# State-space products of two blocks in one group, and gate logits as one fp32r pass over stacked rows

## The chip, the core and the metric

The kernel runs on one core of a Trainium2 chip. The time is device microseconds of one execution. Five engines work side by side, each through its own list of instructions in order: TensorE (PE, matmuls), VectorE (DVE), ScalarE (ACT), GpSimd (POOL) and SyncE (SP, which issues most of the transfers).

## The reference, cut to what matters

Two layers over 256 positions of width 1024. The first layer projects its input and mixes two branches: a state-space branch (16 heads of 64, decays within chunks of 128) and a gated linear attention (8 heads, chunks of 64). The second layer is causal softmax attention, since with 256 positions no earlier block exists to be chosen. A final rms norm closes it. All arithmetic is float32.

```python
# state-space branch, layer 1
seg = a_t[..., :, None] - a_t[..., None, :]
decay_ij = jnp.exp(jnp.where(causal, seg, -jnp.inf))
y_diag = jnp.einsum('bcgeij,bcjgep->bcigep', cb[:, :, :, None] * decay_ij, xdt)
y = y_diag + y_off + d_skip[:, :, None] * x_c
# gate of the linear attention, layer 1: gate_lr is 256 x 16, gate_w2 is 16 x 512
log_decay = jax.nn.log_sigmoid(gate_lr @ gate_w2 + gate_b) / GLA_GATE_NORMALIZER
```

## The kernel before, in words

**Gemms.** Each weight piece comes by one transfer from SP into a raw tile `r_` (four buffers, `wraw`), is rounded to fp32r by ACT as `h_` (L78), and DVE takes the rest `l_ = r_ - h_` (L79). A product of float32 accuracy is then three fp32r passes, `mm3`: high by high, high by low, low by high. The tile of a gemm is named by its stage: `pa` (time-major part of layer 1, weights `wa`), `pb` (blocks of 128 features, weights `wb`), `pc` (output projection), `pv`, `pp`, `pf` (layer 2). The input `xT` is scaled and split the same way into `hhi` and `hlo`, one kb (128 of the 1024 inner rows) at a time. Since a raw tile has four buffers, the transfer of the fifth piece waits until the first piece has been read by DVE, and so on: `r_b8`, the ninth piece, waits for `l_a4`.

**Order.** PE's list is written by hand: coroutines (`co_pair`, `co_first`, `co_gla`) sleep for a number of nanoseconds of a virtual clock (`DL`, advanced by `spend`) and their small matmuls are put between two passes of the running gemm when their time has come. On ACT, DVE, POOL and SP a scheduler of the framework sets the order.

**State-space pairs.** `co_pair(blk)` handles one block of 128 features (two heads). It transposes the block (`xtp`), DVE multiplies by dt (`xdt`), `ab` spreads the cumulated decays over 128 partitions, ACT makes the decays `e` (two Relu operations per head, one Exp), POOL cuts the triangle and DVE multiplies by `cbT`. After a second delay come the products `yp`: eight passes of a 128x64 array shape, since they run in plain float32 (two passes for each of four calls) and the two heads fill 64 columns each. DVE then writes `y` from `yp`. The attention of layer 2 has products of the same shapes, `ao`, in which two pairs share one tile.

**Gate.** `co_first` transposes the 16 gate columns (`gtp`) into `glT` (DVE) and later multiplies: `lg0` and `lg1`, four passes each, from 16 rows. Around `lg0` stand `act` (two transposes from 16 rows) and `cb` (from 64 rows).

**PSUM.** The small tiles (`pm`: `xtp`, `ab`, `yp`, `lg`, `gs`, ...) share a pool of four banks. A new tile takes the bank that a reader has left, so its first matmul waits for the reads of an earlier tile.

Of the kernel before, what the change touches and what calls it, by code (L numbers as in the profile page):

```python
# [9 lines left out]
F32 = mybir.dt.float32  # L10
F32R = mybir.dt.float32r
# [14 lines left out]
AHEAD = 4  # L26

DL = {"ss": 1350, "rb": 5000, "gt": 1500, "ac": 7300, "act": 2600, "lg": 2150, "ln": 2250, "cb": 12400,
      "pair0": 11900, "pair1": 9700, "gla0": 650, "glagap": 3650, "gla1": 3350, "gla2": 8700, "r2": 10000,
      "turn": 4150, "rb1": 4000, "at0": 2600, "at2": 5000, "at1": 3700, "at3": 1800, "gqk": 250}  # L30


# [14 lines left out]
def trunk(ctx, tc, xT_d, x_d, cst_d, mat_d, gw2_d, fn_d, wa_d, wb_d, wc_d, wv_d, wp_d, wf_d, out_d):  # L47
# [132 lines left out]
    xT = big.tile([P, KB, T], F32, name="xT", tag="xT")  # L180
    cst = cpool.tile([P, C_N], F32, name="cst")
    mat = cpool.tile([P, M_N], F32, name="mat")
    gw2 = big.tile([16, 512], F32, name="gw2", tag="s4")
    nc.scalar.dma_start(cst, cst_d)
    j = 0
    for k0, n_ in CUTS_A0:
# [2 lines left out]
            raws.append(fetch(src, kbs, cols, "_".join(str(q_) for q_ in k_)))  # L189
        j += 1  # L190
    nc.sync.dma_start(mat, mat_d)
    nc.sync.dma_start(gw2, gw2_d)

    ident = mat[:, M_ID:M_ID + P]
    tri = [mat[:, M_TRI + P * i:M_TRI + P * i + P] for i in range(2)]
# [113 lines left out]
    ahl = cpool.tile([P, T], F32R, name="ahl")  # L309
    sel = cpool.tile([P, 16], F32R, name="sel")  # L310
    G.memset(ahl.bitcast(F32), 0.0)
    glT = cpool.tile([16, T], F32, name="glT")
    gab = big.tile([P, 4, T], F32, name="gab", tag="s0")
    gmn = big.tile([P, 4, T], F32, name="gmn", tag="s1")
    gcs = big.tile([P, 16, 64], F32, name="gcs", tag="s2")
# [2 lines left out]
    def co_first(ps):  # L318
# [45 lines left out]
        for b2 in range(2):  # L364
            lg = pm(f"lg{b2}")
            for j in range(2):
                b = 2 * b2 + j
                mm(lg[:, j * T:j * T + T], gw2[:, b * P:b * P + P], glT)
            for j in range(2):
                b = 2 * b2 + j  # L370
                gbc = cst[:, C_GB + b:C_GB + b + 1]
                S.activation(gab[:, b, :], lg[:, j * T:j * T + T], AF.Abs, bias=gbc)
                V.tensor_scalar(gmn[:, b, :], lg[:, j * T:j * T + T], gbc, 0.0, op0=ALU.add, op1=ALU.min)
            yield DL["lg"]
# [16 lines left out]
    def co_conv(blk, ps):  # L391
        while "rb" not in env:
            yield 100
        pd = pads[blk % 2]
        V.tensor_tensor(pd[:, 4:4 + T], ps, rb, op=ALU.mult)
        u = tmp.tile([P, T], F32, name=f"cu{blk}", tag="t1a")
        w = lambda i: cwh[:, 4 * blk + i:4 * blk + i + 1]
        S.activation(u, pd[:, 4:4 + T], AF.Identity, scale=w(3), bias=cwh[:, 40 + blk:41 + blk])
        for i in range(3):
            V.scalar_tensor_tensor(u, pd[:, 1 + i:1 + i + T], w(i), u, op0=ALU.mult, op1=ALU.add)  # L400
        th = tmp.tile([P, T], F32, name=f"cth{blk}", tag="t1b")
        S.activation(th, u, AF.Tanh)
        dst = xs[:, blk, :] if blk < 8 else bc[:, blk - 8, :]
        V.scalar_tensor_tensor(dst, th, 1.0, u, op0=ALU.add, op1=ALU.mult)
        if blk < 8:
            spawn(co_pair(blk))
        elif blk == 9:
            spawn(co_cb())

# [11 lines left out]
            S.activation(sb, ps[:, 0:3 * P], AF.Copy)  # L421
            cbT.append(sb)

    def co_pair(blk):
        yield DL["pair0"]
        tp = pm(f"xtp{blk}")
        for tt in range(2):
            tr(tp[:, tt * P:tt * P + P], xs[:, blk, tt * P:tt * P + P])
        xdt = tmp.tile([P, 2, 2, 64], F32, name=f"xdt{blk}", tag="t1c")
        V.tensor_tensor(xdt, tp[:, 0:T].rearrange("p (a b c) -> p a b c", a=2, b=2),  # L430
                        dt[:, :, 2 * blk:2 * blk + 2][:, :, :, None].to_broadcast([P, 2, 2, 64]), op=ALU.mult)
        e = tmp.tile([P, 2, 3, P], F32, name=f"e{blk}", tag="t3")
        for j in range(2):
            h = 2 * blk + j
            ab = pm(f"ab{h}")
            mm(ab[:, 0:T], sel[:, h:h + 1].to_broadcast([P, P]), ahl)
            S.activation(e[:, j, 0:2, :].rearrange("p a b -> p (a b)"), ab[:, 0:T], AF.Relu, scale=-1.0,
                         bias=acs[:, 0, h:h + 1])
            S.activation(e[:, j, 2, :], ab[:, P:T], AF.Relu, scale=-1.0, bias=acs[:, 1, h:h + 1])
        ef = e.rearrange("p a b c -> p (a b c)")  # L440
        S.activation(ef, ef, AF.Exp, scale=-1.0)
        for j in range(2):
            G.affine_select(out=e[:, j, 0:3:2, :], in_=e[:, j, 0:3:2, :], pattern=[[0, 2], [1, P]],
                            compare_op=ALU.is_ge, fill=0.0, base=0, channel_multiplier=-1)
        V.tensor_tensor(e, e, cbT[blk // 4].rearrange("p (a b) -> p a b", a=3)[:, None, :, :].to_broadcast([P, 2, 3, P]),
                        op=ALU.mult)
# [3 lines left out]
        for j, r in enumerate(rows):  # L450
            mm(yp[r, 0:T], xdt[:, 0, j, :], e[:, j, 0:2, :].rearrange("p a b -> p (a b)"), True, False)
        for j, r in enumerate(rows):
            mm(yp[r, P:T], xdt[:, 1, j, :], e[:, j, 2, :], False, True)
        V.scalar_tensor_tensor(y[:, blk, :], xs[:, blk, :], cst[:, C_DS + blk:C_DS + blk + 1], yp[:, 0:T],
                               op0=ALU.mult, op1=ALU.add)
# [451 lines left out]
```

## Time and profile before

| | |
|---|---|
| median of 3 runs | 346.22 us (346.11 to 346.32) |
| profiled execution, its own time | 345.89 us |
| span, first to last instruction | 344.2 us |
| PE busy | 334.2 us (97%) |
| DVE busy | 262.4 us (76%) |
| ACT busy | 217.4 us (63%) |
| POOL busy | 51.3 us (15%) |

Busy is the time in which an engine had at least one instruction under way. The span leaves out what lies ahead of the first and behind the last instruction, 1.7 us of the execution's own time. Matmuls are pipelined: what one costs is the step from its start to the start of the next, not its length.

### The profile page before, as it was taken

The page shows a single profiled execution, that of the slowest core. Times are in us where ns is not written, and L with a number is a line of the kernel's source. Part 1 is how long each engine was busy: PE and PEld are TensorE (multiplying, and loading weights), DVE is VectorE, ACT ScalarE, POOL GpSimd, SP SyncE. Part 2 cuts the span into 40 slices and gives each one's busy share as a digit, 9 for nine tenths or more (in the row PEclk, how much of TensorE's full clock was granted, in tenths as well). Part 3 has the DMA queues.
Part 4 walks back from the last instruction along what each step waited for, and adds up shares of the span by engine and source line. Part 5 has one row for each costly group of instructions (what it writes and reads, how often), then busy time and mean ns, then how long its engine had stood idle before and what let it go on. Part 6 is the DMA issues. An engine that isn't in the chain of part 4 may idle for free.

```text
span 344.2 us, 6316 instructions
## 1 busy us (share of the span) xinstructions
PE 334.2 (97%) x2352; PEld 306.3 (89%) x2352; DVE 262.4 (76%) x548; ACT 217.4 (63%) x445; POOL 51.3 (15%) x62
## 2 busy tenths in 40 slices
PE   7989999999999999999999999999999999999992
PEld 6989899998999899999888888899998999998792
DVE  4979999999989667789965765556867968778352
ACT  5547789898765757677542766464674856746331
POOL 2540001112405442534210000000000000000000
PEclk9999999999999999999999999999999999999998
DMA  6978673366572744631686435747544364430003
GB/s 187 268 245 299 229 231 100 89 181 174 161 238 97 263 129 168 204 92 39 202 285 239 164 134 193 237 154 235 171 150 155 120 186 127 138 109 0 2 8 115
DMA packets 17631, 56.09 MB, mean 163 GB/s; under 512 B 2096, under 2 KB 4144, under 8 KB 17472
## 3 DMA queue, kind: packets, MB, share of 16 engines
q1 hardware_dynamic: 16880, 53.53, 48.8%
q10 hardware_dynamic: 720, 2.16, 1.9%
q8 instruction: 18, 0.29, 0.3%
q14 instruction: 13, 0.11, 0.1%
HBM read 54.63 MB, written 1.05 MB: 162 GB/s over the span
## 4 chain that ended last, share of the span: by engine, by line
PE 85%; DVE 4%; issue 4%; DMA 3%; POOL 2%; ACT 1%; SPq 1%; POOLq 0%; DVEq 0%
PE pp L159 20%; PE pb L159 18%; PE pc L159 13%; PE pa L159 11%; PE pv L159 6%; PE pf L159 4%; DMA r_a<-in_wa 3%; PE yp L159 2%; PE ao L159 2%; PE as L159 2%; PE ptp L163 2%; PE gs L159 1%; PE go L159 1%; POOL rr L538 1%; POOL sT L518 1%
## 5 line engine op out<-in xcount | busy, mean ns | idle before, releaser
L159 PE MATMUL pb<-hhi,h_b 128*128 128x256 f32 x208 | 60.0, 288 | 0.0
L159 PE MATMUL pb<-hhi,l_b 128*128 128x256 f32 x208 | 58.9, 283 | 0.8 <-DVE l_b L79 0.8
L159 PE MATMUL pb<-hlo,h_b 128*128 128x256 f32 x208 | 58.8, 282 | 0.0
L159 PE MATMUL pp<-h1hi,h_p 128*128 128x256 f32 x192 | 55.5, 289 | 0.0
L159 PE MATMUL pp<-h1lo,h_p 128*128 128x256 f32 x192 | 54.3, 283 | 0.0
L159 PE MATMUL pp<-h1hi,l_p 128*128 128x256 f32 x192 | 54.3, 283 | 0.0
L79 DVE TENSOR_TENSOR l_p<-r_p,h_p 128x1024 fp32r<-128x1024 f32 x24 | 29.4, 1223 | 18.0 <-ACT h_p L78 17.7
L159 PEld LDWEIGHTS pb<-hhi,h_b 128*128 128x128 f32 x208 | 39.7, 191 | 1.2 <-issue 1.1
L159 PEld LDWEIGHTS pb<-hhi,l_b 128*128 128x128 f32 x208 | 39.8, 191 | 1.0 <-DVE l_b L79 1.0
L159 PEld LDWEIGHTS pb<-hlo,h_b 128*128 128x128 f32 x208 | 39.8, 191 | 0.0
L159 PEld LDWEIGHTS pp<-h1hi,h_p 128*128 128x128 f32 x192 | 36.7, 191 | 1.1 <-issue 0.5
L159 PEld LDWEIGHTS pp<-h1lo,h_p 128*128 128x128 f32 x192 | 36.8, 192 | 0.0
L159 PEld LDWEIGHTS pp<-h1hi,l_p 128*128 128x128 f32 x192 | 36.7, 191 | 0.0
L79 DVE TENSOR_TENSOR l_b<-r_b,h_b 128x1024 fp32r<-128x1024 f32 x26 | 33.0, 1276 | 1.8 <-ACT h_b L78 1.8
L78 ACT ACTIVATE h_p<-r_p 128x1024 fp32r<-128x1024 f32 x24 | 25.4, 1057 | 13.8 <-PE pp L159 7.4
L78 ACT ACTIVATE h_b<-r_b 128x1024 fp32r<-128x1024 f32 x26 | 27.4, 1067 | 8.0 <-DMA r_b<-in_wb 5.6
L159 PE MATMUL pa<-l_a,hhi 128*128 128x416 f32 x80 | 28.9, 361 | 1.3 <-DVE l_a L79 1.3
L159 PE MATMUL pa<-h_a,hhi 128*128 128x416 f32 x80 | 29.6, 370 | 0.0
L159 PE MATMUL pa<-h_a,hlo 128*128 128x416 f32 x80 | 28.7, 359 | 0.0
L79 DVE TENSOR_TENSOR l_a<-r_a,h_a 128x832 fp32r<-128x832 f32 (+1 forms) x24 | 22.4, 945 | 2.4 <-ACT h_a L78 2.4
L78 ACT ACTIVATE h_a<-r_a 128x832 fp32r<-128x832 f32 (+1 forms) x24 | 18.7, 783 | 8.0 <-DMA r_a<-in_wa 6.5
L79 DVE TENSOR_TENSOR l_c<-r_c,h_c 128x1024 fp32r<-128x1024 f32 x16 | 19.9, 1252 | 5.0 <-ACT h_c L78 4.9
(241 smaller groups left out, 804.2 us busy)
## 6 DMA issues: line engine op xcount, KB each, us to landing
r_b<-in_wb SPq DMA_DIRECT2D x26, 512.0 KB, 4.3
r_p<-in_wp SPq DMA_DIRECT2D x24, 512.0 KB, 4.0
r_c<-in_wc SPq DMA_DIRECT2D x16, 512.0 KB, 4.0
r_a<-in_wa SPq DMA_DIRECT2D x16, 416.0 KB, 3.7
r_v<-in_wv SPq DMA_DIRECT2D x8, 512.0 KB, 4.4
r_f<-in_wf SPq DMA_DIRECT2D x8, 512.0 KB, 3.6
r_a<-in_wa SPq DMA_DIRECT2D x8, 208.0 KB, 4.0
xT<-in_xT SPq DMA_DIRECT2D x8, 128.0 KB, 3.8
```

The costliest lines, as they stand in the source:

```text
L78: S.activation(hi, raw, AF.Copy)
L79: V.tensor_sub(lo, raw, hi.bitcast(F32))
L159: TE.matmul(out, lhsT, rhs, start=start, stop=stop)
L163: TE.transpose(out, in_, ident)
L518: G.affine_select(out=sT[:, 0:3:2, :], in_=sT[:, 0:3:2, :], pattern=[[0, 2], [1, P]], compare_op=ALU.is_ge, fill=0.0, base=0, channel_mult ...
L538: G.tensor_tensor(rr, ss, mhalf, op=ALU.pow)
```

## The change

Blocks are now taken in pairs, (0,1), (2,3), (5,4) and (6,7), by the order in which they come. Each pair is prepared block after block (`xtp`, `ab`, `e`), and the eight calls of both (16 passes) then stand in one group on one tile `yp`; the tags of `xdt` and `e` get a third buffer. The gate logits are one fp32r pass per 128 columns: rows 0 to 15 hold the high part of the gate input, rows 32 to 47 its low part, rows 64 to 79 the high part again, against high, high and low weights; the other rows are zero. For that the weights `gw2` are loaded three times from ACT's queue, behind a memset by POOL, and no longer once from SP's. `rb1` uses the tile of `rb`.

```diff
-      "pair0": 11900, "pair1": 9700, ...
+      "pair0": 6100, "pair1": 5200, "pair2": 9700, ...
...
-    gw2 = big.tile([16, 512], F32, name="gw2", tag="s4")
+    gw2 = big.tile([P, 512], F32, name="gw2", tag="s4")
...
-    nc.sync.dma_start(gw2, gw2_d)
+    G.memset(gw2, 0.0)
+    for r0 in (0, 32, 64):
+        nc.scalar.dma_start(gw2[r0:r0 + 16, :], gw2_d)
...
-    glT = cpool.tile([16, T], F32, name="glT")
+    gl3 = cpool.tile([P, T], F32R, name="gl3")
+    gw3 = big.tile([P, 512], F32R, name="gw3", tag="s2")
+    G.memset(gl3.bitcast(F32), 0.0)
...
-        V.tensor_copy(glT, gtp[0:16, 0:T])
+        S.activation(gl3[0:16, :], gtp[0:16, 0:T], AF.Copy)
+        S.activation(gl3[64:80, :], gtp[0:16, 0:T], AF.Copy)
+        V.tensor_sub(gl3[32:48, :], gtp[0:16, 0:T], gl3[0:16, :].bitcast(F32))
+        S.activation(gw3, gw2, AF.Copy)
+        V.tensor_sub(gw3[64:80, :], gw2[64:80, :], gw3[64:80, :].bitcast(F32))
...
-                mm(lg[:, j * T:j * T + T], gw2[:, b * P:b * P + P], glT)
+                mm(lg[:, j * T:j * T + T], gw3[:, b * P:b * P + P], gl3)
...
-            spawn(co_pair(blk))
+            if "xs" in env:
+                spawn(co_pair(env.pop("xs"), blk))
+            else:
+                env["xs"] = blk
...
-    def co_pair(blk):
-        yield DL["pair0"]
+    def co_pair(*blks):
...
+        for i, blk in enumerate(blks):
+            yield DL[f"pair{i}"]
...
-        yield DL["pair1"]
-        yp = pm(f"yp{blk}")
...
+        yield DL["pair2"]
+        yp = pm(f"yp{blks[0]}")
+        for n, (e, xdt) in enumerate(zip(es, xds)):
+            for j, r in enumerate(rows):
+                mm(yp[r, n * T:n * T + T], xdt[:, 0, j, :], e[:, j, 0:2, :].rearrange("p a b -> p (a b)"), True, False)
+            for j, r in enumerate(rows):
+                mm(yp[r, n * T + P:n * T + T], xdt[:, 1, j, :], e[:, j, 2, :], False, True)
```

How it moves instructions is seen at three places. On PE, the products of block 1 stood alone with the preparation of block 3 behind them (`xtp_998`, `ab_1004`, `ab_1008`; the number behind a name tells tiles apart):

```order
421 L159 MATMUL pb_976<-hlo,h_b_826 128x256
422 L159 MATMUL pb_976<-hhi,l_b_827 128x256
423 L159 MATMUL yp_992<-e_848,xdt_846 64x256 x2
424 L159 MATMUL yp_992<-e_848,xdt_846 64x128 x2
425 L163 MATMUL xtp_998<-mat,xs 128x128 x2
426 L159 MATMUL ab_1004<-ahl,sel 128x256
427 L159 MATMUL ab_1008<-ahl,sel 128x256
428 L159 MATMUL pb_976<-hhi,h_b_826 128x256
```

Now those of blocks 0 and 1 stand together, ahead of the same preparation:

```order
435 L159 MATMUL pb_1019<-hhi,l_b_886 128x256
436 L159 MATMUL yp_1026<-e_767,xdt_765 64x256 x2
437 L159 MATMUL yp_1026<-e_767,xdt_765 64x128 x2
438 L159 MATMUL yp_1026<-e_860,xdt_858 64x256 x2
439 L159 MATMUL yp_1026<-e_860,xdt_858 64x128 x2
440 L163 MATMUL xtp_1037<-mat,xs 128x128 x2
441 L159 MATMUL ab_1043<-ahl,sel 128x256
442 L159 MATMUL ab_1047<-ahl,sel 128x256
443 L159 MATMUL pb_1019<-hhi,h_b_885 128x256
```

The group of block 0, which stood alone some 60 rows earlier, is gone from there. Behind the preparation of block 3 come 24 passes of `pb` and then the preparation of block 5 (`xtp_1087`); before, 45 passes and a group of products stood between the two:

```order
465 L159 MATMUL pb_1080<-hlo,h_b_925 128x256
466 L159 MATMUL pb_1080<-hhi,l_b_926 128x256
467 L163 MATMUL xtp_1087<-mat,xs 128x128 x2
468 L159 MATMUL ab_1093<-ahl,sel 128x256
469 L159 MATMUL ab_1097<-ahl,sel 128x256
```

Four banks hold `yp_1026`, `xtp_1037`, `ab_1043` and `ab_1047`. The program has `xtp_1087` wait for ACT's reads of `ab_1043`, `ab_1093` for those of `ab_1047`, and `ab_1097` for the second `y` from `yp_1026`.

The third place is the start, on DVE, where the scheduler's order differs. Before (`hhi` and `hlo` are the split input, `l_a_4` the fifth weight piece's low part):

```order
5 L324 TENSOR_SCALAR cwh<-cst 128x50
6 L216 SCALAR_TENSOR_TENSOR hlo<-xT,cst,hhi 128x256
7 L79 TENSOR_TENSOR l_a_0_155<-r_a_0_113,h_a_0_154 128x416
8 L216 SCALAR_TENSOR_TENSOR hlo<-xT,cst,hhi 128x256
9 L79 TENSOR_TENSOR l_a_1_161<-r_a_1_116,h_a_1_160 128x416
10 L215 TENSOR_SCALAR hhi<-xT,cst 128x256
11 L79 TENSOR_TENSOR l_a_2_167<-r_a_2_119,h_a_2_166 128x416
12 L216 SCALAR_TENSOR_TENSOR hlo<-xT,cst,hhi 128x256 x2
13 L79 TENSOR_TENSOR l_a_3_173<-r_a_3_122,h_a_3_172 128x416
14 L215 TENSOR_SCALAR hhi<-xT,cst 128x256
15 L79 TENSOR_TENSOR l_a_4_179<-r_a_4_125,h_a_4_178 128x416
16 L216 SCALAR_TENSOR_TENSOR hlo<-xT,cst,hhi 128x256 x2
```

And now:

```order
6 L218 SCALAR_TENSOR_TENSOR hlo<-xT,cst,hhi 128x256
7 L217 TENSOR_SCALAR hhi<-xT,cst 128x256
8 L79 TENSOR_TENSOR l_a_0_158<-r_a_0_113,h_a_0_157 128x416
9 L218 SCALAR_TENSOR_TENSOR hlo<-xT,cst,hhi 128x256
10 L79 TENSOR_TENSOR l_a_1_164<-r_a_1_116,h_a_1_163 128x416
11 L218 SCALAR_TENSOR_TENSOR hlo<-xT,cst,hhi 128x256
12 L79 TENSOR_TENSOR l_a_2_170<-r_a_2_119,h_a_2_169 128x416
13 L218 SCALAR_TENSOR_TENSOR hlo<-xT,cst,hhi 128x256
14 L79 TENSOR_TENSOR l_a_3_176<-r_a_3_122,h_a_3_175 128x416
15 L217 TENSOR_SCALAR hhi<-xT,cst 128x256
16 L218 SCALAR_TENSOR_TENSOR hlo<-xT,cst,hhi 128x256 x2
17 L79 TENSOR_TENSOR l_a_4_182<-r_a_4_125,h_a_4_181 128x416
```

The `hhi` of the third kb (row 7, from the third `xT` transfer) now stands ahead of `l_a_0`, and the two `hlo` of row 16 stand ahead of `l_a_4`, where they stood behind it. On SP's queue the third `xT` transfer now waits for a transfer counter that `cst` used (the three `gw2` loads use three of the eight counters), where it waited for nothing, and `mat` is issued ahead of `r_b8` and `r_b9` instead of behind them.

## Rows read from the trace of the kernel before

**Rows 1.** The page: busy us of each engine, its share of the span, instructions.

```profile
PE 334.2 (97%) x2352; PEld 306.3 (89%) x2352; DVE 262.4 (76%) x548; ACT 217.4 (63%) x445; POOL 51.3 (15%) x62
```

**Rows 2.** What PE waited for: us in total, times, longest.

```profile
PE pa L159 <- DVE l_a L79: 1.3, 2, 0.7
...
PE pb L159 <- DVE l_b L79: 0.8, 1, 0.8
```

**Rows 3.** PE's timeline around one block's products (start us, us, engine, line, operation).

```profile
63.59 0.28 PE L159 MATMUL pb<-hhi,l_b 128*128 128x256 f32 x1
63.80 0.87 PE L159 MATMUL yp<-e,xdt 128*64 128x256 f32 x8
64.60 0.39 PE L159 MATMUL pb<-hhi,h_b 128*128 128x256 f32 x1
64.82 0.28 PE L159 MATMUL pb<-hlo,h_b 128*128 128x256 f32 x1
64.94 0.28 PE L159 MATMUL pb<-hhi,l_b 128*128 128x256 f32 x1
```

**Rows 4.** PE's timeline in layer 2, around products of two pairs in one group.

```profile
258.24 0.28 PE L159 MATMUL pp<-h1hi,l_p 128*128 128x256 f32 x1
258.45 1.52 PE L159 MATMUL ao<-pT,va 128*64 128x256 f32 x16
259.90 0.39 PE L159 MATMUL pp<-h1hi,h_p 128*128 128x256 f32 x1
260.13 0.28 PE L159 MATMUL pp<-h1lo,h_p 128*128 128x256 f32 x1
```

**Rows 5.** PE's timeline around the second pair of gate logits.

```profile
44.91 0.28 PE L159 MATMUL pb<-hhi,l_b 128*128 128x256 f32 x1
45.11 1.12 PE L159 MATMUL lg<-glT,gw 16*128 16x256 f32 x4
46.17 0.38 PE L159 MATMUL pb<-hhi,h_b 128*128 128x256 f32 x1
46.39 0.28 PE L159 MATMUL pb<-hlo,h_b 128*128 128x256 f32 x1
```

**Rows 6.** PE's timeline around the first pair of gate logits.

```profile
41.81 0.29 PE L361 MATMUL act<-mat,acT 16*128 16x16 f32 x2
41.96 1.10 PE L159 MATMUL lg<-glT,gw 16*128 16x256 f32 x4
42.99 0.93 PE L159 MATMUL cb<-bc 64*128 64x256 f32 x8
```

**Rows 7.** SP's queue at the start (a row's length is that of its issues).

```profile
2.65 0.43 SPq L187 DMA_DIRECT2D xT<-in_xT  x1
...
11.02 3.45 SPq L72 DMA_DIRECT2D r_b<-in_wb  x2
```

**Rows 8.** DVE's timeline at the start; in brackets the idle time before, and its releaser.

```profile
3.96 0.35 DVE L215 TENSOR_SCALAR hhi<-xT,cst 128x256 fp32r<-128x256 f32 x1 [2.75 <-DMA cst<-in_cst]
...
4.35 0.49 DVE L216 SCALAR_TENSOR_TENSOR hlo<-xT,cst,hhi 128x256 fp32r<-128x256 f32 x1
...
10.91 2.69 DVE L216 SCALAR_TENSOR_TENSOR hlo<-xT,cst,hhi 128x256 fp32r<-128x256 f32 x2
...
17.31 3.97 DVE L79 TENSOR_TENSOR l_b<-r_b,h_b 128x1024 fp32r<-128x1024 f32 x2
```

**Rows 9.** The page's groups: busy, mean ns, idle before; the low parts of all `b` pieces.

```profile
L79 DVE TENSOR_TENSOR l_b<-r_b,h_b 128x1024 fp32r<-128x1024 f32 x26 | 33.0, 1276 | 1.8 <-ACT h_b L78 1.8
```

**Rows 10.** PE's timeline, the `ab` pair of block 3.

```profile
73.42 0.48 PE L159 MATMUL ab<-ahl,sel 128*128 128x256 f32 x2
```

**Rows 11.** ACT's timeline: first and last of the four reads of that pair.

```profile
76.71 0.46 ACT L437 ACTIVATE e<-ab,acs 128x256 f32<-128x256 f32 x1
...
77.67 0.38 ACT L439 ACTIVATE e<-ab,acs 128x128 f32<-128x128 f32 x1
```

**Rows 12.** DVE's timeline: `y` of the products that stand ahead of that pair.

```profile
76.27 0.48 DVE L454 SCALAR_TENSOR_TENSOR y<-xs,cst,yp 128x256 f32<-128x256 f32 x1
```

More of the change, by code (lines that the diff above doesn't have):

```diff
@@ L28 @@
 DL = {"ss": 1350, "rb": 5000, "gt": 1500, "ac": 7300, "act": 2600, "lg": 2150, "ln": 2250, "cb": 12400,
-      "pair0": 11900, "pair1": 9700, "gla0": 650, "glagap": 3650, "gla1": 3350, "gla2": 8700, "r2": 10000,
+      "pair0": 6100, "pair1": 5200, "pair2": 9700, "gla0": 650, "glagap": 3650, "gla1": 3350, "gla2": 8700, "r2": 10000,
       "turn": 4150, "rb1": 4000, "at0": 2600, "at2": 5000, "at1": 3700, "at3": 1800, "gqk": 250}
@@ L422, in co_cb @@
             cbT.append(sb)
-    def co_pair(blk):
-        yield DL["pair0"]
[L426 to L446, printed above, removed]
-        yield DL["pair1"]
-        yp = pm(f"yp{blk}")
-        rows = [slice(64 * j, 64 * j + 64) for j in range(2)]
[L450 to L455, printed above, removed]
@@ new lines, in co_pair @@
+    def co_pair(*blks):
+        rows = [slice(64 * j, 64 * j + 64) for j in range(2)]
+        es, xds = [], []
+        for i, blk in enumerate(blks):
+            yield DL[f"pair{i}"]
+            tp = pm(f"xtp{blk}")
+            for tt in range(2):
+                tr(tp[:, tt * P:tt * P + P], xs[:, blk, tt * P:tt * P + P])
+            xdt = tmp.tile([P, 2, 2, 64], F32, name=f"xdt{blk}", tag="t1c", bufs=3)
+            V.tensor_tensor(xdt, tp[:, 0:T].rearrange("p (a b c) -> p a b c", a=2, b=2),
+                            dt[:, :, 2 * blk:2 * blk + 2][:, :, :, None].to_broadcast([P, 2, 2, 64]), op=ALU.mult)
+            e = tmp.tile([P, 2, 3, P], F32, name=f"e{blk}", tag="t3", bufs=3)
+            for j in range(2):
+                h = 2 * blk + j
+                ab = pm(f"ab{h}")
+                mm(ab[:, 0:T], sel[:, h:h + 1].to_broadcast([P, P]), ahl)
+                S.activation(e[:, j, 0:2, :].rearrange("p a b -> p (a b)"), ab[:, 0:T], AF.Relu, scale=-1.0,
+                             bias=acs[:, 0, h:h + 1])
+                S.activation(e[:, j, 2, :], ab[:, P:T], AF.Relu, scale=-1.0, bias=acs[:, 1, h:h + 1])
+            ef = e.rearrange("p a b c -> p (a b c)")
+            S.activation(ef, ef, AF.Exp, scale=-1.0)
+            for j in range(2):
+                G.affine_select(out=e[:, j, 0:3:2, :], in_=e[:, j, 0:3:2, :], pattern=[[0, 2], [1, P]],
+                                compare_op=ALU.is_ge, fill=0.0, base=0, channel_multiplier=-1)
+            V.tensor_tensor(e, e, cbT[blk // 4].rearrange("p (a b) -> p a b", a=3)[:, None, :, :]
+                            .to_broadcast([P, 2, 3, P]), op=ALU.mult)
+            es.append(e)
+            xds.append(xdt)
+        yield DL["pair2"]
[5 more added lines that the diff above has]
+                mm(yp[r, n * T + P:n * T + T], xdt[:, 1, j, :], e[:, j, 2, :], False, True)
+        for n, blk in enumerate(blks):
+            V.scalar_tensor_tensor(y[:, blk, :], xs[:, blk, :], cst[:, C_DS + blk:C_DS + blk + 1],
+                                   yp[:, n * T:n * T + T], op0=ALU.mult, op1=ALU.add)
@@ L660, in trunk @@
     rq = cpool.tile([P, 2], F32, name="rq")
-    rb1 = cpool.tile([P, T], F32, name="rb1")
+    rb1 = rb
     def co_norm():
@@ L756, in trunk @@
                 ps = gemm_fm(("p", 3 * pr + i), h1hi, h1lo, f"pp{pr}_{i}")
-                t_ = tmp.tile([P, T], F32, name=f"qk{pr}_{i}", tag=("t1a", "t1c")[i])
+                t_ = tmp.tile([P, T], F32, name=f"qk{pr}_{i}", tag=("t1a", "t1c")[i], bufs=2 + i)
                 n_ = (P, T)[i]
```

## The prediction

> **What bounds the kernel now.** I read the page's busy times first: PE has an instruction under way for 334.2 us of the 344.2 us span, 97%, the next engine is DVE with 76% [rows 1]. Then the waits of PE, since a busy engine can still be a late one: in all it waits 1.3 us for `l_a` (twice) and 0.8 us for `l_b` (once) [rows 2], and these lie in the first 20 us, where weights arrive one by one. From there on the kernel is as long as PE's list. So whatever the change takes out of PE's list is a gain, whatever it adds to DVE, ACT and POOL costs nothing as long as PE does not come to wait for it, and the two places where it might are the start and the four PSUM banks.
>
> **What the products save.** The price of a group is read as the step from the pass ahead of it to a pass behind it, less the steps that would stand there anyway. Steady `pb` passes lie 0.12 us apart (64.82 to 64.94). For one block: from 63.59 to 64.82 is 1.23 us, less two steps of 0.12, 0.99 us for eight passes [rows 3]. Passes of the same shapes for two pairs in one group stand in layer 2: from 258.24 to 260.13 is 1.89, less 0.24, 1.65 us for sixteen [rows 4]. Two blocks apart cost 1.98 us, together 1.65; 0.33 us saved per pair, four pairs, **1.32 us**. What goes away is one entry and one exit: the pass into the group starts 0.21 us behind its neighbour (63.59 to 63.80) and the one after its exit 0.22 us (64.60 to 64.82), where 0.12 is the rule [rows 3]. The sixteen passes of `ao` are the same in count and shape, so I see no wide error in this term.
>
> **What the logits save.** `lg1` stands alone in a `pb` gemm: 44.91 to 46.39 is 1.48, less 0.24, 1.24 us for four passes from 16 rows [rows 5]. Afterwards it is two fp32r passes of 128 rows and 256 columns, the shape and type of a `pb` pass, so two steps of 0.12: **1.00 us** saved. `lg0` stands between two transposes from 16 rows (`act`) and `cb` from 64 rows: from 41.81 to 42.99 is 1.18 us, of which `act` has 0.15 [rows 6]. Its two passes will cost 0.24, but a shape of 128 rows now comes between one of 16 and one of 64, so there is one entry and exit more; at the 0.33 us that an entry and an exit cost above this makes 0.15 + 0.24 + 0.33 = 0.72 and saves **0.46 us**; without that extra change of shape it would be 0.79, with two of them 0.13. Together PE's list loses 1.32 + 1.00 + 0.46 = 2.78 us.
>
> The Trainium skill, "TensorEngine Tiling (Array Packing)", section "Key Properties", says that changing the tiling mode drains TensorE. That speaks for grouping the products and against the place of the new `lg0`; the entry and exit steps of rows 3 agree with it, and no row here shows a passage from 16 to 128 rows and on to 64. By it the saving at `lg0` is 0.46 us, without it 0.79.
>
> **What the start loses.** The first 20 us are paced by arrivals: DVE begins at 3.96, when `cst` lands, PE runs short of `l_a` twice and of `l_b8` once. Three things move there. First, the third `xT` transfer is issued at 2.65 now [rows 7]; with the eight transfer counters shared with the three `gw2` loads it waits until `cst` has landed, so 3.96 - 2.65 = 1.3 us later [rows 7, 8], and DVE does that part's `hhi` ahead of `l_a_0`, so all low parts start behind it. Secondly, `l_a_4` now stands behind two `hlo`, which took 2.69 us at that place, though a single one took 0.49 elsewhere [rows 8]. `r_b8` is issued only when `l_a_4` is done: at 11.02 now [rows 7]; `mat` goes ahead of it. So `r_b8` is issued later by 1.3 us plus the pair of `hlo`, 0.98 to 2.69. PE already waits for `l_b8`, so this is paid in full, less what comes back: the first two `l_b` take 3.97 us together, 1.98 each [rows 8], where the mean of their kind is 1.28 [rows 9], so if they fall into a quieter stretch each is 0.7 us shorter. Low end: 1.3 later and one `l_b` shorter, 0.6 us. High end: 1.3 + 2.69 less both, 2.6 us. Middle of the road, the pair at its plain price and one `l_b` shorter: 1.3 + 0.98 - 0.7 = 1.58; since the two short waits for `l_a` (1.3 us) can absorb a little of it, I take **1.4 us**. Nothing is late next: PE waits for no low part after this one [rows 2], and a later PE gives the others more time.
>
> **What the banks lose.** Block 5's preparation (`xtp`, then two `ab`) now comes 24 passes behind that of block 3, 24 steps of 0.12 or 2.9 us, where 45 passes and a group stood between. It takes the banks of block 3's `ab` and of the first `yp`. In the trace, `ab` of block 3 begins at 73.42 [rows 10], and ACT reads the pair only from 76.71 to 78.05 [rows 11]: the first is free some 4.0 us after its start (two of four reads), the second 4.6 us. The new preparation comes 0.24 + 2.9 = 3.1 us after that start, so with ACT as late as now PE stands 0.9 us for the first and 1.5 us in all. `y` of the products ahead of that pair ends at 76.75 [rows 12]; now there are two, one more of 0.48, and if one more weight piece of at most 1.28 [rows 9] comes between, the second ends at 78.5, where block 5's last `ab` wants its bank at about 76.9: 1.6 us. But ACT and DVE feed from arrivals and not from PE alone: a PE that is 1.4 us late meets them 1.4 us further on, and 1.4 less 1.4 is nothing. I take **0.6 us** for all waits of this kind (0 to 1.6), the first scores `gs` behind `xdt` of block 7 among them, which follow now without a pass between.
>
> **What costs nothing.** POOL's two memsets, three more small transfers, ACT's four new operations and DVE's subtractions: ACT is busy 63%, POOL 15% [rows 1]; the cover is that PE's list is longer than theirs, and where it is gone is the start, priced above. The third buffers and `rb1` take no time.
>
> **The sum.** -2.78 + 1.4 + 0.6 = -0.8 us. The profiled execution took 345.89 us, span 344.2 and 1.7 around it; that makes 345.1. The median of the three runs is 346.22, 0.33 above the profiled one, so I forecast **345.4 us**, 0.2% faster. A measurement here can tell about 0.2%, 0.7 us, from no change.
>
> **Rivals.** (A) *Part of the gain is kept*: the forecast, 344.7 to 345.9; 0.4. (B) *The whole gain is kept*: the start's issues are later but the 1.3 us of waits for `l_a` and the shorter `l_b` take them up, and the banks are free in time. For it: PE idles 2.1 us at the start already [rows 2]. Against: `l_b8` is the last wait there and its transfer is issued by the event that moves. 346.22 - 2.78 + 0.3 = 343.7 us, to 344.6; 0.22. (C) *Start and banks eat the gain*: the start at 2.0 and the banks at 0.8 us, both within their bounds; 346.2, from 345.9 to 346.9; 0.24. (D) *The start decides for slower*: the pair of `hlo` stays at 2.69 us, the `xT` wait adds 1.3, and the `l_b` are not shorter since POOL's sums move along with them; then `r_b8` is 4.0 us late and PE with it. 346.22 - 2.78 + 4.0 + 0.3 = 347.7 us. The point from which this is slower is a start loss of 2.8 + 0.7 - 0.3 = 3.2 us. For it: the same engine beside POOL took 2.69 us for that pair. Against: the issue then coincides with the time at which it was quiet before; 0.14.
>
> **Range and chances.** To leave out no more than 2 in 10 I go from the good end of B to just short of D: 343.7 to 347.2 us. A alone: 344.7 to 345.9. Faster by over 0.2% (below 345.5): B, and two thirds of A, 0.5. Within 0.2%: the rest of A and most of C, 0.32. Slower: D and an edge of C, 0.18.
>
> **What would show it.** On PE, `yp` as four groups of sixteen passes at 1.65 us from step to step, and `lg1` at 0.24 us without a longer step ahead or behind; `act` to `cb` at 0.72. On SP, `r_b8` issued between 12.5 and 15 us; in PE's waits, the one for `l_b` grown to about 2 us or more and that for the first `l_a` with it, and small new waits at `xtp` or `ab` of block 5, for ACT or DVE. The forecast is wrong if PE's busy time does not fall by about 2.8 us (then the prices of the groups were misread), if the first `pb` waits for less than 1 us (then B) or if `l_b8` is ready later than 23 us (then D).

## The result and the profile after

The changed kernel takes **350.11 us** (348.99 to 352.05, four executions), the kernel before, on the same chip, 346.27 us (346.11 to 347.68): ratio 1.011, interval 1.0083 to 1.0137. It is 1.1% slower; the forecast was 345.4 us, range 343.7 to 347.2. The profiled execution took 348.99 us, span 347.3; 3.1 us more than that of before, and the accounts below are made against this one.

The page's busy line, which answers to [rows 1]:

```profile
PE 332.6 (96%) x2348; PEld 306.0 (88%) x2348; DVE 261.9 (75%) x549; ACT 217.9 (63%) x448; POOL 43.5 (13%) x64
```

PE's busy time fell by 1.6 us while the span grew by 3.1. So PE waits more, and the list of its waits (us in total, times, longest) says where; in [rows 2] there were 1.3 us for `l_a` and 0.8 for `l_b`, and neither `ab` nor `xtp` nor `obt`:

```profile
PE pa L159 <- DVE l_a L79: 3.9, 2, 2.2
...
PE ab L159 <- DVE y L475: 1.2, 1, 1.2
PE obt L163 <- DVE ob L563: 0.8, 1, 0.8
PE xtp L163 <- ACT e L457: 0.5, 1, 0.5
PE ab L159 <- ACT e L457: 0.2, 1, 0.2
PE pa L159 <- ACT h_a L78: 0.2, 1, 0.2
```

The gains came as forecast. PE's timeline at the logits and at one group of products (start, us, operation), against [rows 3, 5, 6]:

```profile
43.60 0.29 PE L371 MATMUL act<-mat,acT 16*128 16x16 f32 x2
43.82 0.50 PE L159 MATMUL lg<-gl,gw 128*128 128x256 f32 x2
44.25 0.93 PE L159 MATMUL cb<-bc 64*128 64x256 f32 x8
...
46.17 0.28 PE L159 MATMUL pb<-hhi,l_b 128*128 128x256 f32 x1
46.29 0.40 PE L159 MATMUL lg<-gl,gw 128*128 128x256 f32 x2
46.53 0.28 PE L159 MATMUL pb<-hhi,h_b 128*128 128x256 f32 x1
...
73.29 0.28 PE L159 MATMUL pb<-hhi,l_b 128*128 128x256 f32 x1
73.50 1.52 PE L159 MATMUL yp<-e,xdt 128*64 128x256 f32 x16
74.95 0.44 PE L163 MATMUL xtp<-mat,xs 128*128 128x128 f32 x2
75.14 0.48 PE L159 MATMUL ab<-ahl,sel 128*128 128x256 f32 x2
```

`act` to `cb` is 0.65 us (1.18 before), `lg1` costs two plain steps, 46.29 to 46.53, and the sixteen products stand together, here with the next preparation behind them; the two groups that stand alone, at 89.24 and 97.69, take 1.65 us each by the steps. Summed over the products (1.31), `lg1` (1.01) and `lg0` (0.53), PE's list is 2.85 us shorter.

The preparation of block 5 follows 24 `pb` passes later. PE's timeline there (in brackets the idle time before, and its releaser):

```profile
78.22 0.28 PE L159 MATMUL pb<-hhi,l_b 128*128 128x256 f32 x1
79.03 0.44 PE L163 MATMUL xtp<-mat,xs 128*128 128x128 f32 x2 [0.53 <-ACT e L457]
79.65 0.38 PE L159 MATMUL ab<-ahl,sel 128*128 128x256 f32 x1 [0.18 <-ACT e L457]
81.19 0.35 PE L159 MATMUL ab<-ahl,sel 128*128 128x256 f32 x1 [1.16 <-DVE y L475]
81.38 0.28 PE L159 MATMUL pb<-hhi,h_b 128*128 128x256 f32 x1
```

From 78.22 to 81.38, less a step, are 3.04 us for a group that costs 0.46 elsewhere in the same trace. What it waits for, on ACT the reads of block 3's `ab`:

```profile
78.27 0.45 ACT L455 ACTIVATE e<-ab,acs 128x256 f32<-128x256 f32 x1
...
79.23 0.37 ACT L457 ACTIVATE e<-ab,acs 128x128 f32<-128x128 f32 x1
```

and on DVE the second `y`, behind two `l_a` and among the operations of a convolution:

```profile
77.52 1.95 DVE L79 TENSOR_TENSOR l_a<-r_a,h_a 128x832 fp32r<-128x832 f32 x2
79.38 0.48 DVE L410 SCALAR_TENSOR_TENSOR cu<-pad,cwh,cu 128x256 f32<-128x256 f32 x1
79.78 0.47 DVE L475 SCALAR_TENSOR_TENSOR y<-xs,cst,yp 128x256 f32<-128x256 f32 x1
80.17 0.48 DVE L410 SCALAR_TENSOR_TENSOR cu<-pad,cwh,cu 128x256 f32<-128x256 f32 x1
80.57 0.47 DVE L475 SCALAR_TENSOR_TENSOR y<-xs,cst,yp 128x256 f32<-128x256 f32 x1
```

The products of that pair stood on PE from 73.50 to 74.95; their second `y` ends at 81.04, six microseconds later. The two `l_a` stand ahead of the first `y`, so that one too is late: it begins 4.64 us behind the `ab` pair of block 3 (75.14), where before it was 2.85 us [rows 10, 12]. The same kind of thing happens at `obt`, in a part that the change does not touch:

```profile
156.62 1.21 DVE L79 TENSOR_TENSOR l_c<-r_c,h_c 128x1024 fp32r<-128x1024 f32 x1
157.75 1.12 DVE L563 SCALAR_TENSOR_TENSOR ob<-go,rr,gs 128x128 f32<-128x128 f32 x4
```

PE's `obt` waits 0.83 us for that `ob`:

```profile
158.40 0.95 PE L163 MATMUL obt<-mat,ob 128*128 128x128 f32 x4 [0.83 <-DVE ob L563]
```

In the trace of before an operation of 0.42 us and no low part stood right ahead of the four `ob`, and PE's `obt`, at 154.52, had no wait:

```profile
153.47 0.42 DVE L592 SCALAR_TENSOR_TENSOR zu<-pb,rb 128x256 f32<-128x256 f32 x1
153.81 1.12 DVE L542 SCALAR_TENSOR_TENSOR ob<-go,rr,gs 128x128 f32<-128x128 f32 x4
```

By the steps that `obt` group takes 1.70 us, before 0.65.

Last the start. DVE's timeline, which answers to [rows 8]:

```profile
7.17 0.35 DVE L217 TENSOR_SCALAR hhi<-xT,cst 128x256 fp32r<-128x256 f32 x1 [2.17 <-DMA xT<-in_xT]
...
17.22 1.65 DVE L359 TENSOR_TENSOR gw<-gw,gw 16x512 fp32r<-16x512 f32 x1
18.90 1.01 DVE L79 TENSOR_TENSOR l_a<-r_a,h_a 128x416 fp32r<-128x416 f32 x1
```

and PE:

```profile
19.96 0.46 PE L159 MATMUL pa<-l_a,hhi 128*128 128x416 f32 x1 [2.16 <-DVE l_a L79]
...
21.25 0.31 PE L159 MATMUL pb<-hhi,l_b 128*128 128x256 f32 x1
```

The third kb's `hhi` waits 2.17 us for its `xT`, and the subtraction of the gate weights stands right ahead of the last `l_a` of the first gemm. The first `pb` pass that needs a low part comes at 21.25, before at 19.67; the second `pa` gemm begins 1.7 us later, and its second pass 1.8 (27.73 against 25.92). The path of the forecast lies close behind: `r_b8` was issued at 14.12, its high part was ready at 19.49 (18.43 and 1.06 us), and with 1.2 us for `l_b` its low part could have come at about 20.7 (an estimate), where it came at about 21.1 behind the late `l_a`.

**The account** of the profiled execution, by steps on PE: list -2.85, start +1.8, banks +3.2 (2.58 at block 5, 0.58 at the first `gs` behind `xdt` of block 7), `obt` +1.05: +3.2 us, measured +3.1.

### The profile page after: what moved, and what is told of

It is laid out like the page before. It is cut to its first block, busy times and chain, and to the rows that moved or that the text cites. A ratio compares the mean times of both kernels' runs of the same rounds, so it can differ in the third digit from the quotient of the medians.

```text
span 347.3 us, 6315 instructions
## 1 busy us (share of the span) xinstructions
PE 332.6 (96%) x2348; PEld 306.0 (88%) x2348; DVE 261.9 (75%) x549; ACT 217.9 (63%) x448; POOL 43.5 (13%) x64
## 3 DMA queue, kind: packets, MB, share of 16 engines
HBM read 54.69 MB, written 1.05 MB: 161 GB/s over the span
## 4 chain that ended last, share of the span: by engine, by line
PE 82%; DVE 8%; issue 4%; DMA 3%; POOL 2%; ACT 0%; POOLq 0%; DVEq 0%
PE pp L159 20%; PE pb L159 17%; PE pc L159 13%; PE pa L159 11%; PE pv L159 6%; PE pf L159 4%; PE ao L159 2%; PE as L159 2%; PE ptp L163 2%; PE yp L159 1%; DVE l_a L79 1%; DVE l_c L79 1%; DMA r_a<-in_wa 1%; PE gs L159 1%; DMA cst<-in_cst 1%
## 5 line engine op out<-in xcount | busy, mean ns | idle before, releaser
L79 DVE TENSOR_TENSOR l_b<-r_b,h_b 128x1024 fp32r<-128x1024 f32 x26 | 31.6, 1222 | 0.6 <-ACT h_b L78 0.6
L78 ACT ACTIVATE h_c<-r_c 128x1024 fp32r<-128x1024 f32 x16 | 16.9, 1057 | 9.8 <-DMA r_c<-in_wc 6.5
```

The costliest lines, as they stand in the source:

```text
L78: S.activation(hi, raw, AF.Copy)
L79: V.tensor_sub(lo, raw, hi.bitcast(F32))
```

## The experiments

Two causes are to be told apart. **Timing**: the shorter list is real, and the loss comes from where the preparations stand against ACT's and DVE's lists. **Start**: the loss comes from the gate weights' loads and their split in the first 20 us. The expectations number their theories: in theory 1 both stand side by side; in theory 2 the late start upsets ACT and DVE and the later waits follow from it; theory 3, from `e6_before_again` on, has the start vary with what DVE does beside POOL. Ratios are against the kernel before on the same chip; microseconds of different runs can come from different chips.

**The two halves.** `e1_pairs` takes the pairs alone, `e2_logits` the logits alone.

```diff
# e1_pairs, against the kernel before
-            spawn(co_pair(blk))
+            if "xs" in env:
+                spawn(co_pair(env.pop("xs"), blk))
...
# e2_logits, against the kernel before
-                mm(lg[:, j * T:j * T + T], gw2[:, b * P:b * P + P], glT)
+                mm(lg[:, j * T:j * T + T], gw3[:, b * P:b * P + P], gl3)
```

> The changed kernel with the gate logits as before, so only the pairing of blocks is left. Theory 1 (three separate causes: the start loses 1.8 us through the loads and the split of the gate weights, the four PSUM banks lose about 3.2 us and the last obt 1.0 us through the pairing): PE list 1.31 us shorter, start as before, PE waits 1 to 3 us before ab of block 5 for ACT and DVE; 0.9 to 2.9 us slower than before (ratio 1.003 to 1.008). Theory 2 (the late start alone upsets ACT and DVE, and the later waits follow from it): no wait at ab and obt, 1.3 us faster (0.996).

> The kernel before with the new gate logits alone, blocks one by one. Theory 1: PE list 1.54 us shorter, the start as late as in the changed kernel (1.8 us), no bank wait; 0.3 us slower, within 0.3 to either side (0.999 to 1.002). Theory 2: the start is 1.8 us late and bank waits follow, 2 us or more slower (1.006 or more).

`e1_pairs`: 348.33 us, 1.0042 (1.0021 to 1.0062). PE waits 1.0 us at `ab` for `y` and 0.9 at `obt`; its small groups in layer 1 (all that stands between passes of gemms, by the steps) sum to 31.4 us, where before they took 29.8, so the pairs alone lose 1.6 us between them although their products are 1.3 shorter. `e2_logits`: 347.2 us, 1.0006 (0.9989 to 1.0022); the groups fall to 28.3, and the start gives the 1.4 us back: 4.0 us of waits for `l_a`. Its start is late (`act` at 45.34, before at 41.81) and no wait at `ab` or `obt` follows, which speaks against theory 2. But `e1_pairs`, with loads and gate as before, waits 3.3 us for `l_a` as well: a late start does not need the gate weights. Both causes hold a part. The halves sum to 1.0048, less than the 1.011 of the whole.

**Where the loads are issued.** The three `gw2` loads go back to SP's queue behind `mat`, with the logits alone and with the whole change.

```diff
-        nc.scalar.dma_start(gw2[r0:r0 + 16, :], gw2_d)
+        nc.sync.dma_start(gw2[r0:r0 + 16, :], gw2_d)
```

> As the logits alone, but the three loads of the gate weights are issued by SP behind mat, so the split of the weights falls behind the start. Both theories: start as before, no new wait, 1.3 to 1.6 us faster (0.9955 to 0.9963). If the price at the start is the split on DVE itself and not its place, it is no faster than before.

> The changed kernel with the three loads issued by SP behind mat. Theory 1: start as before, bank waits and obt stay (up to 4.2 us), PE list 2.85 us shorter: 0 to 1.5 us slower than before (1.000 to 1.004), 1.8 to 3 us faster than the changed kernel. Theory 2: no waits left, 2.8 us faster than before (0.992).

347.47 us, 1.001 (0.9989 to 1.003), and 350.05 us, 1.0082 (1.0055 to 1.011): no different from the same kernels with ACT's queue; `e5_after_sp` waits 1.4 us at `xtp` for `y`, 0.8 at `obt` and, by the steps, 0.6 at `gs`. The same times hide a move. In `e5_after_sp` the first `pb` pass with a low part comes at 19.72, as before (19.67; 21.25 in the change), but the second pass of the second `pa` gemm only at 27.25 (25.92 before, 27.73 in the change): the split of the gate weights, later now, stands right ahead of that gemm's first pieces on ACT and DVE. In `e3_logits_sp` DVE's order at the start is that of before, and PE waits 4.1 us for `l_a`, in part at the same place. So the queue looks to have its part in the late start (the runs with squares on ACT, below, show it), and changing it alone gains nothing, since the split then delays PE a little later.

**Both kernels again**, unchanged, to see how steady the start is.

> The kernel before once more, for a second profile. If the start of the first profile (first pb pass at 18.5 us, one long wait for l_a) is typical, it comes again within 0.3 us and the ratio is 1.000. Theory 3 (the start is a matter of which DVE operations fall beside POOL's squares and sums, and that differs with the arrivals from run to run): the first pb pass moves by up to 2 us, and other l_a than in the first profile take 1.2 to 1.7 us instead of 0.58.

> The changed kernel once more, for a second profile. With a fixed loss (theory 1) the subtraction of the gate weights takes 1.6 us again ahead of the last l_a, PE waits 3.9 us for l_a, 1.9 us at the banks, 0.8 at obt; ratio 1.008 to 1.012. By theory 3 the waits for l_a move by 1 to 2 us between the two profiles while banks and obt stay.

346.78 us, 1.0008 (0.999 to 1.0026), and 349.85 us, 1.0095 (1.0072 to 1.0117), with the bank waits (1.2 at `ab`, 0.9 at `xtp`) and that at `obt` (0.8) as in the first profile. With the list of before, PE waits 2.5 us for `l_a` in this profile, where [rows 2] have 1.3. DVE and POOL of `e6_before_again`:

```profile
10.98 1.68 DVE L79 TENSOR_TENSOR l_a<-r_a,h_a 128x416 fp32r<-128x416 f32 x1
...
14.66 1.67 DVE L79 TENSOR_TENSOR l_a<-r_a,h_a 128x416 fp32r<-128x416 f32 x1
```

```profile
10.87 1.34 POOL L227 TENSOR_TENSOR xsq<-xsq 128x512 f32<-128x512 f32 x1
14.42 3.94 POOL L227 TENSOR_TENSOR xsq<-xsq 128x512 f32<-128x512 f32 x3 [2.21 <-ACT xsq L223]
```

Both `l_a` begin just behind a sum of POOL and end 0.45 and 0.6 us behind that sum's end (12.21, and 14.42 plus a third of 3.94 is 15.73). Which of DVE's operations meets a sum differs from run to run.

**Without POOL's squares and sums** (of the first norm's mean square, which is left out; ACT's two squares fill its place), in both kernels.

```diff
-            G.tensor_tensor(sq, src, src, op=ALU.mult)
...
-        G.tensor_tensor(xsq[:, a:a + n_, :], xsq[:, a:a + n_, :], xsq[:, b:b + n_, :], op=ALU.add)
+    S.activation(xsq[:, 0:2, :], xT[:, 2:4, :], AF.Square)
+    S.activation(xsq[:, 2:4, :], xT[:, 6:8, :], AF.Square)
```

> The kernel before without POOL's squares and sums of the input (the mean square of the first norm is left out, its place filled by a part of the squares); DVE's order is the same. Theory 3: every l_a takes 0.58 us, the two l_b 1.2 each, PE waits less than 1 us for them, 0.5 to 2 us faster than before (0.994 to 0.9985), and runs spread less than 1 us. If POOL is not the cause, the same as before with the same spread.

> The changed kernel with the same work left out. Theory 3: the subtraction of the gate weights takes about 0.4 us, the last l_a is no longer late, and the start differs from that of the kernel before without sums by at most the 1.2 us by which the third part of xT is issued later; banks and obt still cost 4 us against 2.85 saved, so 1 to 2.5 us slower than that kernel (about 1.000 to 1.004 of before). Theory 1: as far behind that kernel as the changed one is behind the kernel before (3 us or more).

`e8_before_nosum`: 344.03 us, 0.993 (0.9905 to 0.9954). Every `l_a` now takes 0.59 us:

```profile
10.64 0.59 DVE L79 TENSOR_TENSOR l_a<-r_a,h_a 128x416 fp32r<-128x416 f32 x1 [0.24 <-ACT h_a L78]
...
13.22 0.58 DVE L79 TENSOR_TENSOR l_a<-r_a,h_a 128x416 fp32r<-128x416 f32 x1
```

`e9_after_nosum`: 349.2 us over the six executions that the ratio counts, 1.0064 (1.0034 to 1.0093): still slower than the kernel before, with the subtraction of the gate weights at 0.68 us and the wait for `l_a` down to 1.6. The waits at `xtp`, `ab` (1.2) and `obt` (1.2) stay. The two kernels stay 1.3% apart: POOL's sums delay the start, but they are not why the change is slower. With POOL out of the way the start shows the forecast's own path. `r_b8` is issued at 13.73, in `e8_before_nosum` at 11.26, and the first `pb` pass comes 2.46 us later (19.30, 16.84), with these waits in the changed kernel (0.6 and 0.8 us at the same places in `e8_before_nosum`):

```profile
19.30 0.38 PE L159 MATMUL pb<-hhi,h_b 128*128 128x256 f32 x1 [0.68 <-ACT h_b L78]
20.56 0.39 PE L159 MATMUL pb<-hhi,l_b 128*128 128x256 f32 x1 [0.76 <-DVE l_b L79]
```

In this profile something was added to the bank wait (window, its us, busy us and count of PE, PEld, DVE, ACT, POOL, granted clock, DMA share, GB/s):

```profile
78.00:80.70 2.70, 1.08 (x4) 0.67 (x5) 2.70 (x6) 2.65 (x5) 0.77 (x2) 0.96 0.62 189
80.70:82.00 1.30, 1.30 (x7) 1.30 (x7) 1.30 (x3) 1.12 (x4) 0.00 (x0) 0.50 0.73 283
82.00:84.00 2.00, 2.00 (x12) 2.00 (x11) 2.00 (x5) 2.00 (x5) 0.00 (x0) 0.52 0.01 3
84.00:86.00 2.00, 2.00 (x19) 2.00 (x19) 2.00 (x2) 1.82 (x3) 1.44 (x2) 1.00 0.21 63
```

PE is busy 1.08 of 2.70 us, then the granted clock is half for 3.3 us (1.2 of 2.4 GHz): 15 passes stand 0.21 apart, not 0.12, 1.4 us. In the first profile of the change the same wait left it at 1.00.

**Each block prepared at its own time**, so that only the products stay together. `e13_after_spread` is otherwise the change; `e10_spread_sp` adds loads by SP and a later `obt`, `e11_spread_sp_sq` squares by ACT.

```diff
+      "pair0": 10000, "pair2": 8700, ...
...
+        yield DL["pair0"]
...
+            made.append((blk, e, xdt))
+        if len(made) < 2:
+            return
+        blks, es, xds = zip(*made)
+        made.clear()
+        yield DL["pair2"] + (1500 if blks[0] == 6 else 0)
# e10_spread_sp and e11_spread_sp_sq besides
-        yield DL["gla2"]
+        yield DL["gla2"] + (1500 if b == 3 else 0)
```

> The changed kernel with its start unchanged, but each block prepared at its own time (delay 10000 behind its convolution, products 8700 behind the second block's preparation, 10200 for the last pair), so that no bank is wanted sooner after its last use than in the kernel before; the groups of 16 stay. If the bank waits are the larger part of the loss (theory 1 and 3): no wait at xtp, ab and gs (3.2 us), no fall of the clock behind them (up to 1.4 us), obt stays at 0.8 to 1: 346 to 347, 0.5 us slower than before to 0.5 faster (0.9985 to 1.0015), 3 to 4 us faster than the changed kernel. If the late start upsets the later stages (theory 2): still 1.007 or more.

> As that one, with the loads of the gate weights from SP's queue behind mat (start as before) and the last obt 1500 of the virtual clock later. No wait at banks nor at obt, PE list 2.85 us shorter: 343.7 to 344.5, 0.5 to 0.8 percent faster than before (0.992 to 0.995), if the start is the same on average. If the start stays later by chance of DVE beside POOL: 0.996 to 0.999.

> As that one, with all four squares of the first norm on ACT and only the three sums on POOL. If DVE operations beside POOL set the start (theory 3), POOL's time at the start falls from 10.7 to about 8 us, fewer l_a are stretched, and it is another 0.5 to 1.5 us faster (0.989 to 0.993). If ACT's two more squares delay h_a, it is 0.3 us slower than without.

349.21 us, 1.0081 (1.0062 to 1.01); 349.41 us, 1.0089 (1.0067 to 1.0111); 347.67 us, 1.0042 (1.002 to 1.0064): none has the gain that was expected. The waits for banks are gone, though in `e13_after_spread` the start is as late as in the change, so they did not follow from it; the one at `obt` is gone too with the later time. A new one took their place, in `e10_spread_sp`:

```profile
PE xtp L163 <- DVE xs L414: 3.7, 5, 1.9
```

At 10000 ns PE comes for `xs` before DVE has made it. Too early costs about as much as too close together.

**Squares by ACT alone**, and delays per block: `e12_before_sq` (before), `e16_after_sq` (the change), `e15_logits_sq` (logits alone, loads by SP), `e17_pairs_sq` (pairs alone, mended delays), `e14_all` (all of it).

```diff
-        if k4 % 2:
-            S.activation(sq, src, AF.Square)
-        else:
-            G.tensor_tensor(sq, src, src, op=ALU.mult)
+        S.activation(sq, src, AF.Square)
# e17_pairs_sq and e14_all besides, on e10_spread_sp's form
+        yield {5: 12600, 4: 13300, 7: 10000}.get(blk, 11900)
+        yield DL["pair2"] + (4400 if blks[0] == 6 else 0)
```

> The kernel before with all four squares on ACT, as a control for the last one: what this alone gives. Theory 3: 0.5 to 1.5 us faster than before (0.9957 to 0.9985); without an effect of POOL on DVE: 1.000.

> The changed kernel with nothing but all four squares on ACT. If the loss of the changed kernel lies in the banks, obt and the gate weights at the start: all of these stay, so it is 2.5 to 4.5 us slower than the kernel before with squares on ACT (346.9 to 348.9, 1.001 to 1.007). If it lay only in DVE beside POOL: within 1 us of that kernel (0.994 to 0.997).

> The new gate logits with loads from SP's queue behind mat, blocks one by one, all four squares on ACT; DVE's order at the start is that of the kernel before with the squares on ACT, which was at 344.4. If logits alone save their PE time once the start is the same: 1.5 us below that, 342.9 (0.9895 to 0.992 of before). If the build of the weights costs it again elsewhere: 344 or more.

> Paired products alone, logits as before, squares on ACT, delays set so that neither a bank nor an xs is wanted earlier than in the kernel before (block preparation 11900, for block 5 12600, 4 13300, 7 10000; products 8700, last pair 13100; last obt 1500 later). No wait behind the start: 344.4 - 1.31 - 0.26 at obt = 342.8 (0.989 to 0.992). If pairing itself costs more than its delays: 344 or more, with waits at xtp, ab or yp.

> Both parts of the change with these delays, loads from SP's queue, squares on ACT. If gains add: 344.4 - 1.54 - 1.31 - 0.26 = 341.3 (0.985 to 0.988), no wait behind the start longer than 0.3 us. If a faster PE list only meets ACT and DVE earlier: 342.5 to 344 with waits at xtp for xs or ab.

| run | us | ratio (interval) |
|---|---|---|
| `e12_before_sq` | 344.39 | 0.9946 (0.9929 to 0.9962) |
| `e16_after_sq` | 349.94 | 1.0107 (1.0078 to 1.0136) |
| `e15_logits_sq` | 344.61 | 0.9954 (0.9931 to 0.9976) |
| `e17_pairs_sq` | 342.94 | 0.9898 (0.9878 to 0.9918) |
| `e14_all` | 343.44 | 0.9917 (0.9895 to 0.9939) |

`e16_after_sq` is 5.5 us behind `e12_before_sq`, but the start is not quiet in it: in the profiled executions, 4.0 us apart, PE reaches `act` 3.4 us later (44.36, 40.93). `r_b8` is issued at 12.99 there, at 11.62 in `e12_before_sq`, PE waits 1.1 us for `h_b` and 0.8 for `l_b`, and the granted clock is 0.50 from 20.6 to 23.9. With the loads by SP (`e15_logits_sq`, `e14_all`) `r_b8` is issued at 11.14 and 11.31, and the first `pb` pass with a low part comes at 18.0, not at 20.87. So the place of the loads is a part of the loss. The other part is the timing: the pairs alone, with mended delays, are 1.4 us faster than `e12_before_sq`, and their small groups sum to 27.9 us where those of `e12_before_sq` take 29.7; in `e1_pairs`, the same products with the delays of the change, the sum had risen by 1.6. The waits of `e17_pairs_sq`, all there are beside the warm-up:

```profile
PE pb L159 <- DVE l_b L79: 0.8, 1, 0.8
PE pa L159 <- DVE l_a L79: 0.4, 1, 0.4
```

The logits bring nothing measurable in either kernel, though PE's list is 1.5 us shorter with them. In `e14_all` they are given back by `act`, which PE reaches 1.5 us later than in `e17_pairs_sq` (41.64, 40.10), for the most part at the second `pa` gemm (its second pass starts 1.17 us behind its first):

```profile
24.49 0.46 PE L159 MATMUL pa<-h_a,hhi 128*128 128x416 f32 x1 [0.24 <-ACT h_a L78]
25.66 0.46 PE L159 MATMUL pa<-l_a,hhi 128*128 128x416 f32 x1 [0.71 <-DVE l_a L79]
```

because the split of the gate weights stands ahead of that gemm's first pieces on ACT and DVE.

**The split later.** `e18_all_late` is `e14_all` with the weights loaded and split after that point; `e19_repaired` is the same with the squares shared by POOL and ACT as in the change.

```diff
...
         yield DL["rb"]
+        for r0 in (0, 32, 64):
+            nc.sync.dma_start(gw2[r0:r0 + 16, :], gw2_d)
...
         V.tensor_sub(ahl[32:48, :], acT, ahl[0:16, :].bitcast(F32))
+        S.activation(gw3, gw2, AF.Copy)
+        V.tensor_sub(gw3[64:80, :], gw2[64:80, :], gw3[64:80, :].bitcast(F32))
```

> Both parts with the mended delays and squares on ACT, and the gate weights loaded from SP's queue only behind the first four pieces of the second pa gemm and split later, so that this split no longer stands ahead of that gemm's first h and l on ACT and DVE (where PE waited 1.2 us with the earlier loads). If that place was all that held the logits' gain back: 341.2 to 341.8 (0.984 to 0.987 of before), 1.2 to 2 us under the paired products alone. If the gain is lost to later arrivals: 342.5 to 343.5.

> The same with the squares shared between POOL and ACT as in the kernel before, so that only the parts of the change and their timing differ from before; DVE's order at the start is that of the kernel before. If both parts gain what PE's list says: 3.1 us faster than before (0.990 to 0.993), with the start's spread of before. If the squares alone made the difference: 0.998 to 1.001.

342.97 us, 0.9892 (0.9863 to 0.992), and 343.71 us, 0.992 (0.9888 to 0.9951). The wait at the second `pa` gemm is gone in `e18_all_late`, but it is no faster than `e17_pairs_sq`: PE still reaches `act` 0.9 us later (41.01), and behind it meets ACT and DVE at other places:

```profile
43.92 0.50 PE L159 MATMUL lg<-gl,gw 128*128 128x256 f32 x2
...
71.41 0.44 PE L163 MATMUL xtp<-mat,xs 128*128 128x128 f32 x2
72.02 0.38 PE L159 MATMUL ab<-ahl,sel 128*128 128x256 f32 x1 [0.17 <-DVE xdt L441]
```

`lg1` costs 0.56 instead of 0.24 and the group at 69.78 2.67 instead of 2.05. `e19_repaired` is the change with other delays and with later loads and split of the gate weights, nothing else: 0.8% faster than before, with PE's only wait past the warm-up the 3.0 us for `l_a`. `e17_pairs_sq` and `e18_all_late` are 1.0 to 1.1% faster than the kernel before.

## Why the prediction was wrong

- **What the products save**, 1.32 us: measured 1.31. Right, and the borrowed price of `ao` (1.65) was exact.
- **What the logits save**, 1.00 and 0.46: measured 1.01 and 0.53. Right. `act` and two plain steps make 0.39 of the 0.65 us from `act` to `cb`, so the extra entry and exit cost 0.26, not 0.33. The Trainium skill, "TensorEngine Tiling (Array Packing)", section "Key Properties", has the drain at a change of tiling; by it the saving was to be 0.46, without it 0.79, and the trace's 0.53 speaks for it.
- **What the start loses**, 1.4: measured 1.8. The size was near, the path only in part, so the nearness is luck. `r_b8` was issued at 14.12, inside the band forecast, but PE did not wait for `l_b` at all; its last wait, 2.16 us, was for `l_a`, behind the gate weights' subtraction (called free under "What costs nothing"), which took 1.65 us beside POOL. The forecast's path stood about half a microsecond behind (the estimate above), and where POOL is out of the way it sets the start: 2.46 us from `e8_before_nosum` to `e9_after_nosum`. How the 1.8 us divide between the two is not shown; `e1_pairs`, with loads and gate as before, has a late start too.
- **What the banks lose**, 0.6, bound 1.6: measured 3.2. **This is the step that failed**, twice. The bound left the first `y` at its place and put one weight piece, at the mean of its kind (1.28, called "at most"), between the two; DVE had two `l_a` and a convolution step right ahead of the first `y` and another convolution step between them. Counted from the start of block 3's `ab`, the second `y` ended after 5.9 us, not after 5.1. And within the bound the argument that a later PE meets ACT and DVE later, "1.4 less 1.4 is nothing", took 1.0 us off it: ACT read block 3's `ab` from 78.27, 3.1 us behind PE's first writing (75.14), about as late as before (3.3: 76.71 against 73.42). ACT and DVE had moved with PE. The pairs alone show what these waits and `obt` cost: 1.0042 with them (`e1_pairs`), and 0.9898 without them (`e17_pairs_sq`), where the kernel before with the same squares has 0.9946.
- **Not in the sum at all**: `obt`, 1.05 us. The change moved DVE's list 80 us behind the bank wait, in a part that it does not edit; `e1_pairs` has the wait too (0.9), `e2_logits` has not.
- **What is open.** The profiled execution accounts for 3.1 of the 3.8 us between medians. The fall of the clock behind the bank wait, 1.4 us in one profile and absent in four others with that wait, could fill the rest: the longest of the four executions, 352.05 us, has a mean granted clock of 0.980, the others have 0.989 to 0.990. What the other executions waited for is not on record. Nor is it settled why the two halves lose less apart (1.0048 by their sum) than together.

## What to carry to other kernels

A gain in an engine's list is worth its size only if the work that feeds it stays ahead: when small steps are moved closer together, price each shared buffer by the last reader's place in its own engine's list (all that stands ahead of it, not one piece), and allow for no slack that the trace does not show. Then try the same edit at other times before judging it: the same products and logits were 1.1% slower with one set of delays, and 0.8% faster with another and a later split of the gate weights. A further saving of 1.5 us in PE's list (the logits) gave nothing once PE was paced by arrivals at that place.

## What the runs showed of the hardware that was not expected

- DVE beside POOL: a subtraction of two 128x416 inputs took 0.58 us alone and 1.67 and 1.68 beside POOL's sums, the 16x512 one 0.68 and 1.65. It ended about its own duration behind the end of the POOL instruction that had begun ahead of it. The Trainium skill, "SBUF — State Buffer", section "Who interferes with whom", says that a DVE instruction with two SBUF inputs and a GpSimd instruction that reads SBUF exclude each other, the later one being blocked until the first is done; these rows agree. It is the likely reason why the start of one and the same kernel varies: the waits for `l_a` were 1.3 us in one profile of before and 2.5 in another.
- The granted clock fell from 1.00 to 0.50 (2.4 to 1.2 GHz) in the middle of a kernel, behind waits of PE of 1 to 2 us: from 80.7 to 84.0 in `e9_after_nosum` (PE busy 1.08 of the 2.70 us ahead), from 87.1 to 90.4 in `e11_spread_sp_sq` (1.09 of 3.00), and in the first 24 us from 18.5 to 21.8 in `e1_pairs` (2.35 of 4.40). Behind the same bank wait as in `e9_after_nosum` it stayed at 1.00 in the first profile of the change (1.13 of 3.00) and in `e7_after_again` (1.40 of 3.00). So the cost of a wait of this kind can differ by 1.4 us between executions of like kernels.
